# GpSimd's element work moved to ScalarE and VectorE in a hybrid attention layer

## The chip, the cores and the metric

The kernel runs on one core of a Trainium2 chip. The metric is the device time of one execution in microseconds, as the median of several executions. The engines that matter are TensorE (PE in the rows, PEld for its weight loads), VectorE (DVE), ScalarE (ACT), GpSimd (POOL) and SyncE (SP), whose queue issues most DMAs. Every engine runs its own instructions in the order in which they stand in its queue, and waits for others by semaphores.

## The reference

One layer on 1024 tokens of width 2048, in float32. Its parts, cut to what is computed:

```python
xn = rms_norm(h, norm_w)
qkv, z_a, b_raw, a_raw, u_b, v_b, z_b = split(xn @ w_in)
# group A: 8 heads of 128, gated DeltaNet in chunks of 64
q, k, v = split(silu(causal_depthwise_conv(qkv, conv_w)))       # q, k L2-normalised
beta, g = sigmoid(b_raw), -exp(a_log) * softplus(a_raw + dt_bias)
o_a = rms_norm(chunk_gated_delta_rule(q, k, v, g, beta), head_norm_w) * silu(z_a)
# group B: 8 groups of 128, gMLP in chunks of 128
v_n = layer_norm(v_b, sgu_ln_w, sgu_ln_b)
o_b = u_b * chunked_causal_sgu(v_n, w_spatial, b_spatial) * silu(z_b)
return rms_norm(h + concat(o_a, o_b) @ w_out, final_norm_w)
```

Inside a chunk the DeltaNet needs the decay mask exp(gc_i − gc_j), where gc is the running sum of g, and k, v scaled per token.

## The kernel before

**Halves and stages.** The tokens are done in two halves of 512. Each half runs `group_a` (four pairs of heads, with the recurrence of the state) and then `group_b` (eight channel groups); after both, `out_phase` does the output projection in seven products of half-size blocks, which need four sums and differences of the quarters of w_out. These are made ahead, once for each half's share, by `w_sums`, eight rounds in each `group_b`: four loads (`ws`), four VectorE operations (L833, L834, L836, L837) and four stores to the DRAM tile `wc_d`.

**Projection.** TensorE gets float32 accuracy from three products of high and low parts (L238, L239, L241). Weights come in chunks of 128 x 512: a DMA on SP's queue into `wr` (3 buffers), a cast on ScalarE into `wh` (L136, 4 buffers), a subtraction on VectorE into `wl` (L137, 4 buffers), then 12 matmuls of 512 columns. A tile is four chunks; `acc` is its sum. In the names the numbers tell tile and chunk (`wl_17_3` is chunk 3 of tile 17).

**Tasks.** What follows a tile is written as a generator that `tick()` moves on by a step. `task_gates` makes the decay masks `em` of a half: the running sums go through DRAM (`gcd`) and come back replicated (L389), GpSimd subtracts (L395), VectorE clamps (L397), ScalarE takes the exponential (L398), in four parts. `task_k`, `task_q` and `task_v` convolve (`conv`, L410 and L413), normalise (`rsqrt_`, L127 to L132) and scale per token (`kc` L486, `kd` L488, `bv` L537, em times beta L503). `task_pair` runs the recurrence of a pair, adds the part inside the chunk (`at`, L649 and L650), scales `o` by its norm (L661) and swaps it (`swap`: a 32 x 32 transpose on VectorE L425, four stores L430 and one load L433 through DRAM; for `o` on GpSimd's queue); L672 then multiplies by the gate and the result goes to `mix_d` (L673). `spatial` writes `s` (L746, L749) for group B, `task_u` multiplies it in (L755). `x_load` and its squares (L158, L159) prepare the next half's x. `finish` squares and scales the rows of the output (L950, L952) before the last factor.

**Order and buffers.** A list scheduler puts the instructions of all engines in order, with a model of the times, and takes an instruction as soon as its operands and its buffers are free. The pool `wk` gives buffers by tag, with a number of them (`cv` 3, `bv` 2, `o` 2, `gae` 3): a tile waits until the one that had its buffer before has been read for the last time. So which tag a tile has decides where its load may stand. `sp` and `at` share the two PSUM banks of `gen_bank`; therefore the matmuls at L649 of the second head of a pair wait for L746, which reads `sp`.

## Time and profile before

| | |
|---|---|
| runs | 1775.11, 1778.87, 1783.17 us; median 1778.87 |
| profiled execution | 1779.21 us, of it 1777.5 us span |
| mean granted clock of TensorE | 0.992 |
| TensorE, VectorE, ScalarE, GpSimd busy | 1728.8, 1251.7, 738.5, 263.6 us |
| DMA | 277.99 MB, mean 156 GB/s |

The span is what the profile covers of one execution; 1.7 us lie outside. Shares are averages over the whole span. Engine names in the rows are PE, PEld, DVE, ACT, POOL and SP; an SPq is SP's queue of DMA issues. An idle time is put down to what ended it, in brackets behind `<-`.

### The profile page before, as it was taken

Reading aid. Unit: us, or ns where it says so; the run is one execution under the profiler, and the core shown is the slowest. Engines: PE = TensorE matmul, PEld = TensorE weight load, DVE = VectorE, ACT = ScalarE, POOL = GpSimd, SP = SyncE. Lnnn points to the kernel's source line nnn. Section 1 sums busy time; section 2 is a strip of 40 time slices with the busy share of each in tenths; the row PEclk is TensorE's granted clock in tenths of the full one; section 3 lists DMA queues with packets and bytes.
Section 4 is the critical chain, followed back from the end, with each engine's and each line's share of the span. In section 5 each row is a group of like instructions: output and inputs, shape, how many; then the busy total and the mean of one; then the engine's idle time right before and its main releaser. Section 6 shows DMA issues by size and latency. Waiting matters only on the chain.

```text
span 1777.5 us, 27441 instructions
## 1 busy us (share of the span) xinstructions
PE 1728.8 (97%) x9334; PEld 1456.6 (82%) x9334; DVE 1251.7 (70%) x2945; ACT 738.5 (42%) x1678; POOL 263.6 (15%) x314
## 2 busy tenths in 40 slices
PE   9999999999999999998999999999989999999997
PEld 8778788888997788886878878889878888888885
DVE  7798797987747633757979789793863344767765
ACT  7543544445333222646344444532422234433454
POOL 4110131211201200203012112120020000200211
PEclk9999999999999999999999999999999999999998
DMA  7455445364458734426453645444884466766455
GB/s 239 128 134 145 108 124 144 91 169 133 132 172 260 258 108 126 130 69 153 126 134 92 164 106 149 134 116 117 248 277 133 118 188 199 223 191 193 144 190 190
DMA packets 190046, 277.99 MB, mean 156 GB/s; under 512 B 38064, under 2 KB 70864, under 8 KB 189648
## 3 DMA queue, kind: packets, MB, share of 16 engines
q1 hardware_dynamic: 185216, 263.60, 50.9%
q0 software_dynamic: 4544, 12.62, 3.0%
q8 instruction: 73, 1.20, 0.3%
q14 instruction: 69, 0.57, 0.1%
q10 hardware_dynamic: 144, 0.01, 0.0%
HBM read 220.54 MB, written 55.61 MB: 155 GB/s over the span
## 4 chain that ended last, share of the span: by engine, by line
PE 54%; DVE 9%; DMA 7%; ACT 2%; issue 2%; SPq 0%; POOL 0%; DVEq 0%; ACTq 0%; POOLq 0%
PE oa L1002 12%; PE acc L238 10%; PE acc L241 10%; PE acc L239 10%; PE vb L788 7%; DMA ws<-w_out 1%; DVE wl L137 1%; DVE cv L413 1%; DMA xres<-x_tok 1%; DMA wc_d<-ws 1%; DVE c L914 1%; PE p L621 1%; PE sp L744 1%; DMA wr<-w_in 1%; PE at L649 1%
## 5 line engine op out<-in xcount | busy, mean ns | idle before, releaser
L238 PE MATMUL acc<-xh,wh 128*128 128x512 f32 x1472 | 591.8, 402 | 1.0 <-ACT wh L136 1.0
L241 PE MATMUL acc<-xh,wl 128*128 128x512 f32 x1472 | 576.9, 392 | 7.5 <-DVE wl L137 7.5
L239 PE MATMUL acc<-xl,wh 128*128 128x512 f32 x1472 | 575.8, 391 | 0.0
L136 ACT CAST wh<-wr 128x512 fp32r<-128x512 f32 x368 | 225.7, 618 | 427.7 <-PE acc L239 270.6
L137 DVE TENSOR_TENSOR wl<-wr,wh 128x512 fp32r<-128x512 f32 x368 | 258.2, 704 | 154.2 <-ACT wh L136 151.2
L241 PEld LDWEIGHTS acc<-xh,wl 128*128 128x128 f32 x1472 | 277.1, 188 | 67.0 <-DVE wl L137 9.0
L238 PEld LDWEIGHTS acc<-xh,wh 128*128 128x128 f32 x1472 | 278.0, 189 | 57.7 <-issue 3.0
L239 PEld LDWEIGHTS acc<-xl,wh 128*128 128x128 f32 x1472 | 278.0, 189 | 51.5 <-issue 0.2
L1002 PE MATMUL oa<-who,a 128*128 128x512 f32 x864 | 267.9, 390 | 0.2 <-ACT who L136 0.2
L1002 PEld LDWEIGHTS oa<-who,a 128*128 128x128 f32 x864 | 162.6, 188 | 34.7 <-ACT who L136 0.6
L1002 PE MATMUL oa<-wlo,a 128*128 128x512 f32 x432 | 168.7, 390 | 0.6 <-DVE wlo L137 0.5
L137 DVE TENSOR_TENSOR wlo<-wro,who 128x512 fp32r<-128x512 f32 x108 | 79.4, 738 | 52.7 <-ACT who L136 52.2
L413 DVE SCALAR_TENSOR_TENSOR cv<-pc,cw,cv 128x511 f32<-128x511 f32 (+1 forms) x144 | 109.1, 758 | 9.6 <-ACT cv L410 8.2
L788 PE MATMUL vb<-whvb,xh 128*128 128x256 f32 x384 | 110.5, 288 | 0.0
L788 PE MATMUL vb<-wlvb,xh 128*128 128x256 f32 x384 | 108.6, 283 | 0.0
L788 PE MATMUL vb<-whvb,xl 128*128 128x256 f32 x384 | 108.6, 283 | 0.0
L136 ACT CAST who<-wro 128x512 fp32r<-128x512 f32 x108 | 66.6, 618 | 96.6 <-PE oa L1002 63.7
L1002 PEld LDWEIGHTS oa<-wlo,a 128*128 128x128 f32 x432 | 81.3, 188 | 18.5 <-DVE wlo L137 1.7
L566 DVE TENSOR_TENSOR fst<-fs 32x31 f32<-32x31 f32 (+15 forms) x248 | 89.3, 360 | 4.3
L568 DVE TENSOR_TENSOR fs<-fs,fst 32x31 f32<-32x31 f32 (+15 forms) x248 | 89.0, 359 | 4.1
L625 ACT ACTIVATE o<-p,g_egs 64x128 f32<-64x128 f32 x128 | 46.5, 363 | 84.3 <-DVE vz L624 81.6
L952 POOL TENSOR_TENSOR c<-c,fw 128x512 f32<-128x512 f32 x24 | 37.6, 1596 | 254.6 <-ACT sqh L950 254.6
(245 smaller groups left out, 2379.2 us busy)
## 6 DMA issues: line engine op xcount, KB each, us to landing
wr<-w_in SPq DMA_DIRECT2D x368, 256.0 KB, 3.3
ws<-w_out SPq DMA_DIRECT2D x64, 256.0 KB, 4.0
wc_d<-ws SPq DMA_DIRECT2D x64, 256.0 KB, 3.6
wro<-wc_d SPq DMA_DIRECT2D x64, 256.0 KB, 2.8
ar<-mix_d SPq DMA_DIRECT2D x56, 256.0 KB, 3.5
wrvb<-w_vb SPq DMA_DIRECT2D x48, 256.0 KB, 2.7
wro<-w_out SPq DMA_DIRECT2D x48, 256.0 KB, 2.8
xr<-x_t SPq DMA_DIRECT2D x32, 256.0 KB, 4.2
```

The source lines that it names most:

```text
L136: nc.scalar.copy(hi, src)
L137: nc.vector.tensor_tensor(lo, src, hi.bitcast(F32), op=ALU.subtract)
L238: nc.tensor.matmul(acc, hi[:, kk, :], xh, start=(k == 0), stop=False)
L239: nc.tensor.matmul(acc, hi[:, kk, :], xl, start=False, stop=(last and lo is None))
L241: nc.tensor.matmul(acc, lo[:, kk, :], xh, start=False, stop=last)
L413: nc.vector.scalar_tensor_tensor(cv[:, s:], acc[:, :T - s], w, cv[:, s:], op0=ALU.mult, op1=ALU.add)
L566: nc.vector.tensor_tensor(tv, bc(lu[:, k, k + 1:].unsqueeze(2), [32, n, m]), bc(xu[:, k:k + 1, 0:m], [32, n, m]), op=ALU.mult)
L568: nc.vector.tensor_tensor(xu[:, k + 1:, 0:m], xu[:, k + 1:, 0:m], tv, op=ALU.subtract)
L625: nc.scalar.activation(hd["o"][ra, t, :], pp[rq, :], AF.Copy, scale=gt["egs"][rq, h, t:t + 1])
L788: nc.tensor.matmul(a, l[:, tsl], r[:, k % 2, :], start=fl, stop=sp_, skip_group_check=True)
L952: nc.gpsimd.tensor_tensor(c, c, env["fw"][q], op=ALU.mult)
L1002: nc.tensor.matmul(acc[t], l[:, tsl], r[:, 0, :], start=fl, stop=sp_, skip_group_check=True)
```

## The change

Every operation of GpSimd on whole tiles goes to another engine. A product with one factor per partition and sub-block becomes four ScalarE activations with a scale per partition (`kc`, `bv`, the scaling of `o`). The subtraction ahead of the exponential becomes the bias of the exponential, with a negated copy `ngs` of the sums; the clamp on VectorE comes first, and the exponentials are then 64 of 128 x 64 in place of 8 of 128 x 512. The copy of `kq` into `wq` goes to ScalarE. Products and sums of two operands go to VectorE: half of the squares of x, em times beta, the product of `s` with `rb`, the product of `c` with `fw`. The tiles of `w_sums` change their tags from `cv` and `bv` to `o` and `gae`. GpSimd keeps memsets and DMA issues.

```diff
--- before.py
+++ after.py
@@ -156,7 +156,7 @@
                 nc.scalar.activation(xsq[hf, i], xr, AF.Square)
             else:
                 nc.scalar.activation(xr, xr, AF.Square)
-                (nc.vector, nc.gpsimd)[i].tensor_tensor(xsq[hf, i], xsq[hf, i], xr, op=ALU.add)
+                nc.vector.tensor_tensor(xsq[hf, i], xsq[hf, i], xr, op=ALU.add)
         return (xh, xl), squares
 
     def x_rstd(hf):
@@ -365,6 +365,8 @@
         nc.tensor.matmul(gp[:, 64:128], ones, gh.rearrange("p c k -> p (c k)"), start=True, stop=True)
         gc = sm.tile([P, 32], F32, tag="gs", bufs=1, name=f"gs{hf}")
         nc.scalar.copy(gc, gp[:, 0:32])
+        ngc = sm.tile([P, 32], F32, tag="ngs", bufs=1, name=f"ngs{hf}")
+        nc.scalar.activation(ngc, gp[:, 0:32], AF.Copy, scale=-1.0)
         eg, egs, ekd = g8("eg"), g8("egs"), g8("ekd")
         gam = sm.tile([P, 2, H, NT], F32, tag="gam", bufs=1, name=f"gam{hf}")
         nc.scalar.activation(fl(eg), gc, AF.Exp)
@@ -391,11 +393,12 @@
 
         gt["em"] = []
         for q in range(4):
+
             e4 = em[:, q * 8:(q + 1) * 8, :]
-            nc.gpsimd.tensor_tensor(e4, e4, bc(gc[:, q * 8:(q + 1) * 8].unsqueeze(2), [P, 8, 64]), op=ALU.subtract)
+            nc.vector.tensor_tensor(e4, e4, bc(cap.unsqueeze(1), [P, 8, 64]), op=ALU.min)
+            for a in range(8):
+                nc.scalar.activation(e4[:, a, :], e4[:, a, :], AF.Exp, bias=ngc[:, q * 8 + a:q * 8 + a + 1])
             yield 2 if q == 0 else 16
-            nc.vector.tensor_tensor(e4, e4, bc(cap.unsqueeze(1), [P, 8, 64]), op=ALU.min)
-            nc.scalar.activation(e4, e4, AF.Exp)
             gt["em"].append(e4)
 
 
@@ -483,8 +486,9 @@
         kc = wk.tile([P, NT, P], F32, tag="kc", name=f"kc{hf}_{h}")
         kd = wk.tile([P, NT, P], F32, tag="kd", bufs=3, name=f"kd{hf}_{h}")
         S4 = [P, NT, 4, 32]
-        nc.gpsimd.tensor_tensor(kc.rearrange("p t (b c) -> p t b c", c=32), z,
-                                bc(gt["eg"][:, h, :].unsqueeze(2).unsqueeze(3), S4), op=ALU.mult)
+        for t in range(NT):
+            nc.scalar.activation(kc[:, t, :].rearrange("p (b c) -> p b c", c=32), z[:, t], AF.Copy,
+                                 scale=gt["eg"][:, h, t:t + 1])
         nc.vector.tensor_tensor(kd.rearrange("p t (b c) -> p t b c", c=32), z, bc(ce.unsqueeze(2).unsqueeze(3), S4), op=ALU.mult)
         hd.update(nk=nk, c=cb, kc=kc, kd=kd)
 
@@ -500,10 +504,10 @@
         while len(gt.get("em", ())) <= h // 2 or "kd" not in hd:
             yield 1
         em = gt["em"][h // 2][:, hh * NT:(hh + 1) * NT, :]
-        nc.gpsimd.tensor_tensor(em, em, bc(hd["c"].unsqueeze(2), [P, NT, 64]), op=ALU.mult)
+        nc.vector.tensor_tensor(em, em, bc(hd["c"].unsqueeze(2), [P, NT, 64]), op=ALU.mult)
 
         wq = wk.tile([P, NT, 4, 64], F32, tag="wq", bufs=2, name=f"wq{hf}_{h}")
-        nc.gpsimd.tensor_copy(wq[:, :, 1:3, :], kq[:, 1, :].rearrange("p (t c i) -> p t c i", c=2, i=64))
+        nc.scalar.copy(wq[:, :, 1:3, :], kq[:, 1, :].rearrange("p (t c i) -> p t c i", c=2, i=64))
         yield 1
         ga = gen_bank(f"ga{hf}_{h}").rearrange("p (t i) -> p t i", i=P)
         for t in range(NT):
@@ -534,8 +538,9 @@
         while "nk" not in hd:
             yield 1
         bv = wk.tile([P, NT, P], F32, tag="bv", name=f"bv{hf}_{h}")
-        nc.gpsimd.tensor_tensor(bv.rearrange("p t (b c) -> p t b c", c=32), z, bc(hd["nk"].unsqueeze(2).unsqueeze(3), [P, NT, 4, 32]),
-                                op=ALU.mult)
+        for t in range(NT):
+            nc.scalar.activation(bv[:, t, :].rearrange("p (b c) -> p b c", c=32), z[:, t], AF.Copy,
+                                 scale=hd["nk"][:, t:t + 1])
         hd["bv"] = bv
 
     def task_z(hf, h, st, pr, acc):
@@ -658,7 +663,8 @@
             nc.vector.tensor_scalar(hd["ssq"], hd["ssq"], EPS, EPS * P, op0=ALU.add, op1=ALU.mult)
             nc.vector.tensor_tensor(so, so, hd["ssq"], op=ALU.add)
             rsqrt_(ro, so, [P, NT], f"o{nm}")
-            nc.gpsimd.tensor_tensor(o, o, bc(ro.unsqueeze(2), [P, NT, P]), op=ALU.mult)
+            for t in range(NT):
+                nc.scalar.activation(o[:, t, :], o[:, t, :], AF.Copy, scale=ro[:, t:t + 1])
             yield W_SO0
             y = hd["ut"].rearrange("p t d -> p (t d)")
             hd["ot"] = swap(y, o.rearrange("p t d -> p (t d)"), y, f"o{nm}", nc.gpsimd, True)
@@ -746,7 +752,7 @@
         nc.vector.scalar_tensor_tensor(s1, sp, lnw[:, g:g + 1], bc(brow[:, g, :].unsqueeze(1), [P, NT, P]),
                                        op0=ALU.mult, op1=ALU.add)
         s1f = s1.rearrange("p t i -> p (t i)")
-        nc.gpsimd.tensor_tensor(s1f, s1f, sb["rb"], op=ALU.mult)
+        nc.vector.tensor_tensor(s1f, s1f, sb["rb"], op=ALU.mult)
         sb[g] = s1f
 
     def task_u(hf, g, sb, acc):
@@ -827,7 +833,7 @@
         for cb, k in ck:
             q = {}
             for i, b in enumerate(((1, 1), (0, 1), (0, 0), (1, 0))):
-                q[b] = wk.tile([P, 1, T], F32, tag=("cv", "bv")[i // 2], bufs=(3, 2)[i // 2], name=f"ws{cb}_{k}_{i}")
+                q[b] = wk.tile([P, 1, T], F32, tag=("o", "gae")[i // 2], bufs=(2, 3)[i // 2], name=f"ws{cb}_{k}_{i}")
                 nc.sync.dma_start(q[b], w_quarter(b, cb, k))
             yield 5
             nc.vector.tensor_tensor(q[1, 1], q[1, 1], q[0, 1], op=ALU.subtract)
@@ -949,7 +955,7 @@
             sq = wk.tile([P, T], F32, tag="rb", bufs=1, name=f"sqh{n}_{cb}_{t}")
             nc.scalar.activation(sq, c, AF.Square, accum_out=ss[:, q:q + 1])
             if not last:
-                nc.gpsimd.tensor_tensor(c, c, env["fw"][q], op=ALU.mult)
+                nc.vector.tensor_tensor(c, c, env["fw"][q], op=ALU.mult)
                 return
             others = [i for i in range(4) if i != q]
             yield 1
```

In the rows of the changed kernel line numbers are 3 to 6 higher than in the kernel before from the gates on. The numbers at the end of names are the scheduler's and differ between the two.

**SP, during the swap of the last pair of the first half.** `wr` are weights of the projection, `ws` and `wc_d` loads and stores of the sums, `mix_d<-o_3_0` and `mix_d<-o_3_1` what the two heads of the pair store after their swap. Before:

```order
L831 DMA ws_5_2_7000<-w_out 128x512
L831 DMA ws_5_3_7002<-w_out 128x512
L831 DMA ws_6_0_7113<-w_out 128x512
L187 DMA wr_34_0_6365<-w_in 128x512
L840 DMA wc_d<-ws_5_0_6996 128x512
L840 DMA wc_d<-ws_5_1_6998 128x512
L187 DMA wr_34_1_6383<-w_in 128x512
L673 DMA mix_d_132<-o_3_0_5711 128x512
L840 DMA wc_d<-ws_5_2_7000 128x512
```

Changed, around the store of the second head:

```order
L187 DMA wr_42_3_6630<-w_in 128x512
L187 DMA wr_35_0_6649<-w_in 128x512
L679 DMA mix_d_132<-o_3_1_5835 128x512
L187 DMA wr_35_1_6667<-w_in 128x512
L837 DMA ws_0_1_6501<-w_out 128x512
L187 DMA wr_35_2_6689<-w_in 128x512
L846 DMA wc_d<-ws_0_0_6499 128x512
L846 DMA wc_d<-ws_0_1_6501 128x512
L187 DMA wr_35_3_6730<-w_in 128x512
L846 DMA wc_d<-ws_0_2_6503 128x512
L846 DMA wc_d<-ws_0_3_6505 128x512
```

Before, the first head's store stands in the midst of the sixth round of sums; in the changed kernel the first round is stored behind the second head's store, and only four loads of sums stand ahead of that.

**VectorE, around L672 of the first head** (L678 in the changed kernel), whose operand `ut` is the load of the swap. Before:

```order
L137 TENSOR_TENSOR wl_41_0_6287<-wr_41_0_6284,wh_41_0_6286 128x512
L137 TENSOR_TENSOR wl_41_1_6312<-wr_41_1_6309,wh_41_1_6311 128x512
L833 TENSOR_TENSOR ws_5_0_6996<-ws_5_0_6996,ws_5_1_6998 128x512
L834 TENSOR_TENSOR ws_5_1_6998<-ws_5_1_6998,ws_5_2_7000 128x512
L836 TENSOR_TENSOR ws_5_2_7000<-ws_5_2_7000,ws_5_0_6996 128x512
L137 TENSOR_TENSOR wl_41_2_6330<-wr_41_2_6327,wh_41_2_6329 128x512
L672 SCALAR_TENSOR_TENSOR o_3_0_5711<-ut_3_0_5703,hnw,z_6_4785 128x512
L837 TENSOR_TENSOR ws_5_3_7002<-ws_5_3_7002,ws_5_2_7000 128x512
L746 SCALAR_TENSOR_TENSOR s_0_6156<-sp_0_6151,lnw,brow 128x512
L137 TENSOR_TENSOR wl_41_3_6349<-wr_41_3_6346,wh_41_3_6348 128x512
```

Changed:

```order
L137 TENSOR_TENSOR wl_41_1_6410<-wr_41_1_6407,wh_41_1_6409 128x512
L137 TENSOR_TENSOR wl_41_2_6428<-wr_41_2_6425,wh_41_2_6427 128x512
L678 SCALAR_TENSOR_TENSOR o_3_0_5803<-ut_3_0_5795,hnw,z_6_4868 128x512
L752 SCALAR_TENSOR_TENSOR s_0_6251<-sp_0_6246,lnw,brow 128x512
L755 TENSOR_TENSOR s_0_6251<-s_0_6251,rb_715 128x512
L137 TENSOR_TENSOR wl_41_3_6447<-wr_41_3_6444,wh_41_3_6446 128x512
L761 TENSOR_TENSOR s_0_6251<-s_0_6251,acc_32_6037 128x512
L655 TENSOR_TENSOR o_3_1_5835<-o_3_1_5835,at_3_1_6319 128x512
```

The sums `ws_5` are gone from ahead of L672 and from between it and L746 (L752); the product with `rb` stands behind it.

**VectorE, around `wl_17_3` of the second half,** with the masks `em`, the convolved tile `cv_16` and the products `gl`, `gae` of the first pair. Before:

```order
L413 SCALAR_TENSOR_TENSOR cv_16_8533<-pc_16_8531,cw,cv_16_8533 128x509
L514 TENSOR_TENSOR gl_0_8493<-ga_0_8484,em_8327 128x256
L521 TENSOR_TENSOR gae_0_8496<-ga_0_8484,em_8327 64x4x64 x2
L415 SCALAR_TENSOR_TENSOR cv_16_8533<-tails,cw,cv_16_8533 128x3
L137 TENSOR_TENSOR wl_17_3_8545<-wr_17_3_8542,wh_17_3_8544 128x512
L137 TENSOR_TENSOR wl_24_0_8567<-wr_24_0_8564,wh_24_0_8566 128x512
```

Changed, first ahead of `wl_17_3`, then ahead of `wl_24_0`:

```order
L137 TENSOR_TENSOR wl_17_2_8636<-wr_17_2_8633,wh_17_2_8635 128x512
L398 TENSOR_TENSOR em_8427<-em_8427,cap 128x512
L132 SCALAR_TENSOR_TENSOR ce_1_8529<-rst_k_1_8531,ce_1_8529 128x4
L398 TENSOR_TENSOR em_8427<-em_8427,cap 128x512
L130 TENSOR_TENSOR rst_k_1_8531<-ce_1_8529 128x4
L407 TENSOR_TENSOR pc_16_8651<-acc_16_8499,rb_8174 128x512
L131 TENSOR_TENSOR rst_k_1_8531<-rst_k_1_8531,rsm_k_1_8532 128x4
L137 TENSOR_TENSOR wl_17_3_8665<-wr_17_3_8662,wh_17_3_8664 128x512
```

And further on, up to `wl_24_0`:

```order
L525 TENSOR_TENSOR gae_0_8616<-ga_0_8604,em_8427 64x4x64 x2
L507 TENSOR_TENSOR em_8427<-em_8427,cc_1_8528 128x256
L663 TENSOR_SCALAR ssq_0_8621<-ssq_0_8621 128x4
L518 TENSOR_TENSOR gl_1_8705<-ga_1_8696,em_8427 128x256
L525 TENSOR_TENSOR gae_1_8708<-ga_1_8696,em_8427 64x4x64
L416 SCALAR_TENSOR_TENSOR cv_16_8653<-pc_16_8651,cw,cv_16_8653 128x511
L418 SCALAR_TENSOR_TENSOR cv_16_8653<-tails,cw,cv_16_8653 128x1
L416 SCALAR_TENSOR_TENSOR cv_16_8653<-pc_16_8651,cw,cv_16_8653 128x510
L418 SCALAR_TENSOR_TENSOR cv_16_8653<-tails,cw,cv_16_8653 128x2
L416 SCALAR_TENSOR_TENSOR cv_16_8653<-pc_16_8651,cw,cv_16_8653 128x509
L418 SCALAR_TENSOR_TENSOR cv_16_8653<-tails,cw,cv_16_8653 128x3
L137 TENSOR_TENSOR wl_24_0_8687<-wr_24_0_8684,wh_24_0_8686 128x512
```

`wl_17_3` has moved ahead of the convolution and the masks' products; those now stand between it and `wl_24_0`, and two clamps stand ahead of it.

## Rows read from the trace of the kernel before

**Rows 1.** Page part 1: busy us, share of the span, instructions, by engine

```profile
PE 1728.8 (97%) x9334; PEld 1456.6 (82%) x9334; DVE 1251.7 (70%) x2945; ACT 738.5 (42%) x1678; POOL 263.6 (15%) x314
```

**Rows 2.** Timeline of PE around 823 us: start us, length us, instruction [idle before]

```profile
823.09 0.39 PE L238 MATMUL acc<-xh,wh 128*128 128x512 f32 x1
823.32 0.39 PE L239 MATMUL acc<-xl,wh 128*128 128x512 f32 x1
829.28 0.80 PE L241 MATMUL acc<-xh,wl 128*128 128x512 f32 x1 [5.58 <-DVE wl L137]
```

**Rows 3.** Waits of PE: us in total, times, longest us

```profile
PE at L649 <- DVE s L746: 10.7, 2, 5.6
PE acc L241 <- DVE wl L137: 7.5, 3, 5.6
```

**Rows 4.** Windows: busy us of PE, PEld, DVE, ACT, POOL; PEclk, DMA share, GB/s

```profile
575.00:585.00 10.00, 4.93 (x22) 4.53 (x23) 6.81 (x11) 2.75 (x10) 2.20 (x2) 0.66 0.84 280
514.00:604.00 90.00, 83.20 (x468) 71.59 (x467) 66.24 (x160) 31.83 (x81) 13.38 (x15) 0.96 0.80 258
```

**Rows 5.** Timeline around the stop at 574 us: POOL, VectorE and PE

```profile
560.18 1.04 POOL L661 TENSOR_TENSOR o<-o,ro 128x512 f32<-128x512 f32 x1 [83.58 <-DVE ro L132]
572.30 0.57 POOL L433 DMA_DIRECT2D ut<-swapo  x1 [6.64 <-DMA swapo<-ut]
...
560.22 1.54 DVE L833 TENSOR_TENSOR ws<-ws,ws 128x512 f32<-128x512 f32 x1 [0.57 <-DMA ws<-w_out]
577.91 0.75 DVE L672 SCALAR_TENSOR_TENSOR o<-ut,hnw,z 128x512 f32<-128x512 f32 x1 [1.59 <-DMA ut<-swapo]
579.18 0.74 DVE L746 SCALAR_TENSOR_TENSOR s<-sp,lnw,brow 128x512 f32<-128x512 f32 x1
...
580.07 2.05 PE L649 MATMUL at<-ut,gae 128*128 128x128 f32 x8 [5.63 <-DVE s L746]
```

**Rows 6.** The swap's load, L433: timeline row of a quiet pair; landing

```profile
256.62 0.56 POOL L433 DMA_DIRECT2D ut<-swapo  x1 [3.09 <-DMA swapo<-ut]
...
DMA to landing us min/median/max: 2.6/3.4/6.5
```

**Rows 7.** Page part 6, DMA issues: count, KB each, median us to landing

```profile
wr<-w_in SPq DMA_DIRECT2D x368, 256.0 KB, 3.3
ws<-w_out SPq DMA_DIRECT2D x64, 256.0 KB, 4.0
wc_d<-ws SPq DMA_DIRECT2D x64, 256.0 KB, 3.6
```

**Rows 8.** Groups of ACT by line: busy us, mean ns, idle before

```profile
L136 ACT CAST wh<-wr 128x512 fp32r<-128x512 f32 x368 | 225.7, 618 | 427.7 <-PE acc L239 270.6 <-DMA wr<-w_in 82.7 <-issue 31.1
L655 ACT ACTIVATE so<-o 128x128 f32<-128x128 f32 x64 | 19.8, 310 | 24.1 <-DVE rst_o L131 11.9 <-DVE o L650 10.8
L398 ACT ACT_TABLE_LOAD x3 | 3.8, 1283 | 0.1
```

**Rows 9.** Timeline of POOL, VectorE and ACT ahead of the stop at 823 us

```profile
816.93 4.50 POOL L395 TENSOR_TENSOR em<-em,gs 128x512 f32<-128x512 f32 x4 [4.77 <-DMA em<-gcd]
...
818.44 1.00 DVE L132 SCALAR_TENSOR_TENSOR ce<-rst_k,ce 128x4 f32<-128x4 f32 x1
828.54 1.28 DVE L137 TENSOR_TENSOR wl<-wr,wh 128x512 fp32r<-128x512 f32 x2
...
824.10 1.28 ACT L398 ACT_TABLE_LOAD   x1
825.40 0.63 ACT L398 ACTIVATE em<-em 128x512 f32<-128x512 f32 x1
```

**Rows 10.** Groups of VectorE by line: busy us, mean ns

```profile
L159 DVE TENSOR_TENSOR xsq<-xsq,xr 128x512 f32<-128x512 f32 x14 | 9.5, 681 | 0.0
L132 DVE SCALAR_TENSOR_TENSOR ce<-rst_k,ce 128x4 f32<-128x4 f32 x48 | 10.1, 211 | 1.2
```

**Rows 11.** Group of POOL by line: busy us, mean ns, idle before

```profile
L952 POOL TENSOR_TENSOR c<-c,fw 128x512 f32<-128x512 f32 x24 | 37.6, 1596 | 254.6 <-ACT sqh L950 254.6
```

## The prediction

> **What bounds the kernel now.** I read the shares of the engines first, then what TensorE waited for, then the timeline around its longest waits, and last the DMA table. TensorE is busy for 97% of the span, VectorE for 70%, ScalarE for 42% and GpSimd for 15% [rows 1]. In an undisturbed stretch TensorE starts a matmul of 512 columns every 0.23 us [rows 2], so a chunk of a projection tile (12 matmuls) takes 2.76 us, and TensorE sets the time wherever nothing is late. What a change on other engines can win is therefore no more than TensorE's gaps: 1777.5 − 1728.8 = 48.7 us, of which the start and the last chain behind TensorE are untouched here. The list of waits puts names to the largest gaps. Two stops of some 5 us, one in each half, wait for the VectorE step at L746, 10.7 us together, and 7.5 us go to late low parts of weights, 5.6 of them in one stop [rows 3]. A stop costs more than its length, since the granted clock sinks behind it: in the ten microseconds around the first stop TensorE was busy for 4.93 us at a mean granted clock of 0.66 [rows 4], which is 4.93 × 0.34 = 1.7 us lost on top. GpSimd's own 264 us matter only where somebody waits for them or is slowed by them.
>
> **The swap of the last head pair (−13 us).** The first stop is a chain [rows 5]. GpSimd scales o_3_0 at 560.18. VectorE's sum L833 starts beside it, takes 1.54 us where this operation takes about 0.7, and stands ahead of the transpose that starts the swap. The swap goes through DRAM: GpSimd waits 6.64 us for its four stores before it can issue the load at 572.30, and L672, which uses the load, starts 5.61 us later. L746 follows at 579.18 behind L672 and one more sum, and TensorE goes on at 580.07 after a gap of 5.63 us. In a quiet pair the same wait was 3.09 us, and such a load lands in a median 3.4 us [rows 6]. The reason is the DMA load of the sums: between 514 and 604 us the DMA engines are 80% busy at 258 GB/s [rows 4].
>
> The change takes the buffers of the sums from cv and bv, which are free early, and gives them o and gae, which the last pair still holds. In the order of the changed kernel the sums (loads and VectorE work) stand behind this swap, with only a few loads ahead of it. So the wait for stores goes down by 6.64 − 3.4 = 3.2 us (I take 3.4, a load's median, as the upper of the two quiet figures), the load by 5.61 − 3.4 − 0.3 (to start behind it) = 1.9 us, and the two sums that stood in front leave, 0.7 us for each and the 0.8 by which the first was slowed: 7.3 us in all, some 1 us of which the hoisted loads of x and w_out may keep. That exceeds the gap of 5.63. Next late are the weights, whose supply is priced below, and a rest of some 0.5 us per half. The saving: 10.7 + 2 × 1.7 − 2 × 0.5 = 13.1 us. Its bounds are 14 (nothing left) and 6 (the early loads still disturb the swap and half remains).
>
> **The sums behind the swap (+4 us).** This is what the change may cost. Per half there are 32 loads and 32 stores of 256 KB (16.8 MB), and on the same in-order queue of SP stand 25 loads of weights (6.6 MB) among them; before, loads of wrvb stood there too. TensorE eats 25 chunks in 25 × 2.76 = 69 us. For that the DMA would have to move 23.4 MB in 69 us, 339 GB/s. Before, 258 GB/s at 80% busy is 322 GB/s at full share, thus 73 us. Each round of four tiles is also a chain: load 4.0, sums about 1.5 and half a microsecond of issue, store 3.6 [rows 7], some 9.6 us, thus 77 us for eight rounds. Had it gone at 258 GB/s as before, it would be 91 us. Behind a waiting store or load of the sums stand the weights, and for those VectorE's subtraction and TensorE wait. Slack: three raw and four converted chunks, of which six are ahead, 6 × 2.76 = 16.6 us, less landing 3.3 [rows 7], cast 0.6 [rows 8], subtraction 0.7 and 1 of waits, about 11 us. So 73 or 77 us (4 to 8 us behind) cost nearly nothing, and 91 us (22 behind) cost 11 us per half. I take 2 us per half, since the chain of 77 us is the nearest to what the order shows, and single late rounds will be longer than the mean; ends 0 and 22 in all.
>
> **The decay masks of the first pair (−2 us).** The stop of 5.58 us at 829.28 [rows 2] waits for the subtraction wl_17_3, which VectorE started at 828.54. Ahead of it GpSimd's four subtractions ran from 816.93 for 4.5 us, during which VectorE's 128x4 steps took 1.00 us at 818.44 [rows 9] where the mean of that line is 0.21 [rows 10]. After, VectorE has wl_17_3 ahead of the cv steps and is not slowed, so it comes at about 821. But the next subtraction, wl_24_0, stands behind four clamps, two em products, gl, gae and three cv steps: from 817.35 some 12 to 13 us of VectorE work, ending near 830, and TensorE wants it at 823.5 + 2.76 + 0.5 = 826.8. So the stop moves by one tile and shrinks from 5.6 to about 3.5 us. Both VectorE and ScalarE now stand in order behind the landing of em, for which only GpSimd waited. Bounds −6 (no stop) and +3 (em lands later). Switching between tables took 1.28 us here, and the next activation started 1.30 us after the start of the load [rows 9]; eight more switches, mean 1.283 [rows 8], are 10 us of ScalarE, nearly all beside TensorE. The Trainium skill, "ScalarE: Activation LUTs", section "What ACT_TABLE_LOAD costs", adds a drain of 1.38 us to each, 2.66 us in all; the trace does not agree, since no such pause stands between load and activation. By the page this term would be about 0 instead of −2.
>
> **Moved element work, elsewhere (−1 us).** VectorE takes L159 (14 × 0.68 = 9.5 us), the spatial product (16 × 0.68 = 10.9), em times beta (16 at most 0.68, 10.9) and L952 (24 × 0.68 = 16.3, 24 times 1.6 on GpSimd before [rows 11]), 48 us at most, with 0.681 as the mean of the same operation at L159 [rows 10]. Even with nothing given back that is 1300 us, 73%. It gets back what GpSimd's work beside it costs today (the 1.54 at L833, the 1.00 at L132), a like amount by my estimate. ScalarE gets 3 × 16 × 4 = 192 activations of 128x128 (59 us at the 0.310 of L655), 16 copies (10 us), 64 exponentials for 8 (at most 20 us) and 10 us of tables [rows 8]: about 838 us, 47%. The cover is the conversion buffers, some 8 us ahead of TensorE. If ScalarE waits longer than that in order for a swap, the casts behind it are late. For the small gaps in group A I take −1, with bounds −5 and +5.
>
> **The end (+1 us).** In the output phase four of the 24 products stand on VectorE ahead of the last chains, up to 3 × 0.68 = 2 us, of which I take half; the last chain behind TensorE has none. Memsets and the DMA issues of the swap stay on GpSimd, which then is nearly free for them: no cost.
>
> **The sum.** −13 + 4 − 2 − 1 + 1 = −11 us. The profiled run took 1779.2 us (span 1777.5 and 1.7 around it), within 0.3 of the median of 1778.9, so no correction: 1768 us.
>
> **Rivals.**
> *The weights starve behind the sums* (slower). If the eight rounds don't overlap with the weights but follow one another at 12.5 us (the 9.6 us chain and one chunk's load behind it), the stage is 100 us, 31 behind, less 11 of slack, 20 us per half and 1.7 of clock: 43 in place of 4, so 1807 us. From 258 GB/s (91 us) it is 25 in place of 4, 1789. It decides from 10.9 us a round (18 behind, 7 us and 1.7 per half), where the gain is gone. For it speaks that the queue is in order and that 339 GB/s has no row; against it the small number of weights per round (three) and the slack. Chance 0.15.
> *The stop stays in part.* The early loads of x and w_out fill the DMA queues while the swap is under way and half of the saving is lost: −11 + 7 = −4, 1775 us. Chance 0.17.
> *ScalarE becomes the late one.* The bv scaling waits in its queue for the swap of v, and exponentials with tables stand ahead of casts; at half a microsecond for each of 16 heads 8 us are lost, 1776 us. Against it: ScalarE waits for swaps of q and k in the same way today, and its casts spend 270.6 us waiting for TensorE to free their buffers [rows 8], so they have room. Chance 0.13.
> *Everything goes.* No lag, no stop at the first pair and smaller gaps: −13 − 6 − 3 + 1 = −21, 1758 us. Here a page bears: the Trainium skill, "SBUF — State Buffer", section "A bandwidth-pool intuition that's wrong (but worth ruling out)", gives about 358 GB/s between HBM and a core. By that the stage would be 65 us and cost nothing, 1764 us by my sum; the trace shows no stretch at that rate. Chance 0.13.
> *The forecast*, 1762 to 1774 us: chance 0.42.
>
> **How the numbers follow.** Half a per cent, 8.9 us, is about what a measurement of this kernel can tell from no change: faster is below 1770, slower above 1788. Faster: 0.13 and most of the forecast's 0.42 (0.35), with 0.02 from the rest: 0.50. Slower: the first rival beyond 1788, 0.14. Same: 0.36. The range from 1756 to 1788 leaves out the worse part of the first rival and the tail of the best case.
>
> **What would show it.** Right: no stop over 2 us near 574 and 1300 us, the GpSimd wait ahead of the swap's load at 3 to 4 us, sums running from about 575 to 655 us, a stop of 3 to 4 us one tile later at 826 us, VectorE's L132 at 0.16 us there. Wrong: stops of TensorE on wl or wh between 600 and 660 us, with SP waiting for wc_d or ws; new waits on wh in group A behind scaled copies.

## The result, and the profile after

The changed kernel takes 1751.8 us (1750.7 to 1754.2) against 1777.0 us before, a ratio of 0.985 with a 95% interval of 0.983 to 0.987. That is 25 us, where 11 were forecast, and 4 us below the end of the range. The profiled execution took 1754.2 us, its span 1752.5.

Page part 1 of the changed kernel answers to [rows 1]:

```profile
PE 1724.6 (98%) x9334; PEld 1457.0 (83%) x9334; DVE 1222.7 (70%) x3015; ACT 823.5 (47%) x1952; POOL 95.3 (5%) x172
```

GpSimd lost 168 us and ScalarE gained 85. VectorE took over 54 instructions of 128x512 and 16 of 128x256 (some 44 us) and is nonetheless 29 us shorter. Most of what it got back is seen by comparing each of its instructions with the median of its line and shape in the same trace. What instructions take beyond that median, counted where it is over 0.1 us, is called VectorE's excess from here on: before, it adds up to 66.7 us, of which 66.3 fall on instructions that run beside a memset or element instruction of GpSimd; after, it is 0.0.

The waits of TensorE (us in total, times, longest), first two of before that [rows 3] did not show, then the same and two more of the changed kernel:

```profile
PE ds L632 <- DVE vz L624: 4.0, 10, 0.9
PE wp L611 <- DVE wq L612: 2.8, 3, 1.1
```

```profile
PE acc L241 <- DVE wl L137: 11.5, 8, 2.8
PE oa L1008 <- ACT wk L136: 1.1, 1, 1.1
PE ds L637 <- DVE vz L629: 0.6, 3, 0.2
PE wp L616 <- DVE wq L617: 0.6, 1, 0.6
```

The stops for L746 are gone from the list. The many short waits of the recurrence (`ds` for `vz`, `wp` for `wq`) are nearly gone too. The waits for low parts of weights have grown from 7.5 to 11.5 us.

Where the 25 us lie is read by aligning the two traces at the same matmul. The table gives, for the profiled executions, how much longer (+) or shorter (−) a stage is than before; times are those of before, both halves together. The first 55 us and what follows the last matmul are left out (0.7 us at most). Each column is one execution; single executions of the changed kernel lie within 4 us, those of e1 within 15. The row below `rest` is VectorE's excess in group A, in us. The columns to the right are the experiments below.

| stage (us of before) | forecast | after | e1 | e2 | e3 | e9 | e5 | e10 | e6 | e4 | e7 | e8 | e11 | e12 |
|---|---|---|---|---|---|---|---|---|---|---|---|---|---|---|
| masks (85–111, 811–847) | −2 | +1.0 | −1.3 | −1.8 | +1.8 | +0.3 | −6.4 | −1.2 | −1.8 | −0.8 | −0.3 | +5.6 | +4.8 | −2.3 |
| group A (111–532, 847–1259) | −1 | −13.1 | +5.7 | −12.7 | −6.7 | −7.4 | −2.0 | −6.4 | −11.9 | −13.1 | −12.8 | −12.2 | −11.7 | −13.3 |
| swap (532–634, 1259–1350) | −13 | −16.7 | −14.3 | −2.0 | −16.7 | −15.2 | −15.9 | −1.3 | −16.7 | −15.5 | −15.0 | −15.2 | −15.3 | −8.4 |
| sums (634–705, 1350–1434) | +4 | +12.2 | +14.8 | 0.0 | +12.6 | +0.6 | +6.7 | 0.0 | +11.0 | 0.0 | +1.3 | +2.0 | +1.0 | +22.8 |
| output phase (1434 to the last matmul) | +1 | −5.7 | −0.5 | −5.5 | −3.0 | −5.0 | −4.5 | −1.7 | −0.6 | −3.1 | −4.3 | −3.3 | −4.9 | −4.8 |
| rest (55–85, 705–811) | | −3.4 | −0.6 | −3.4 | −3.5 | −3.3 | −2.2 | −1.8 | −3.3 | −3.2 | −3.2 | −3.3 | −2.3 | −3.2 |
| VectorE's excess in A (24.1 before) | | 0.0 | 23.2 | 1.0 | 12.5 | 11.2 | 19.7 | 3.8 | 0.0 | 0.4 | 0.5 | 0.5 | 0.5 | 0.7 |
| **span, profiled** | | 1752.5 | 1781.7 | 1752.7 | 1762.3 | 1748.0 | 1752.9 | 1765.7 | 1754.3 | 1742.3 | 1743.8 | 1751.4 | 1749.0 | 1769.2 |
| **median time** | 1768 | 1751.8 | 1774.8 | 1756.2 | 1758.4 | 1751.0 | 1755.5 | 1766.7 | 1755.8 | 1743.7 | 1746.1 | 1753.1 | 1750.3 | 1770.9 |

**The swap**, timeline of the changed kernel, against [rows 5] (GpSimd, VectorE, TensorE):

```profile
566.27 0.56 POOL L436 DMA_DIRECT2D ut<-swapo  x1 [3.90 <-PE acc L241]
```

```profile
569.60 0.74 DVE L678 SCALAR_TENSOR_TENSOR o<-ut,hnw,z 128x512 f32<-128x512 f32 x1
570.38 0.75 DVE L752 SCALAR_TENSOR_TENSOR s<-sp,lnw,brow 128x512 f32<-128x512 f32 x1
```

```profile
571.28 1.13 PE L654 MATMUL at<-ut,gae 128*128 128x128 f32 x8
```

The wait ahead of the load is 3.90 us instead of 6.64 (it now ends with TensorE's L241, the four stores having landed at 565.61), the multiplication starts 3.3 us behind the load instead of 5.6, nothing stands between it and L752, and TensorE goes through without a stop. The windows of the changed kernel (columns as in [rows 4]) show the clock at 1.00 behind it, and the sums running later at up to 0.87 of DMA share:

```profile
575.00:585.00 10.00, 10.00 (x51) 8.43 (x50) 6.60 (x22) 4.08 (x11) 2.93 (x4) 1.00 0.59 157
600.00:660.00 60.00, 60.00 (x279) 50.14 (x277) 35.47 (x56) 13.60 (x22) 0.00 (x0) 1.00 0.87 284
660.00:680.00 20.00, 16.66 (x65) 13.02 (x64) 9.68 (x16) 3.72 (x6) 0.00 (x0) 0.91 0.79 252
```

**The sums**, VectorE and TensorE around the stop at 664 us:

```profile
664.10 0.69 DVE L839 TENSOR_TENSOR ws<-ws,ws 128x512 f32<-128x512 f32 x1 [4.72 <-DMA ws<-w_out]
666.56 0.69 DVE L137 TENSOR_TENSOR wl<-wr,wh 128x512 fp32r<-128x512 f32 x1
```

```profile
667.30 0.50 PE L241 MATMUL acc<-xh,wl 128*128 128x512 f32 x1 [2.84 <-DVE wl L137]
```

VectorE waits 4.72 us for a load of a sum, in the seventh of the eight rounds, and the subtraction of weights behind it comes at 666.56. The cast of these weights had ended at 661.35. In the second half a stop of 2.76 us stands at the same round.

**The masks in the first half**, VectorE and TensorE:

```profile
90.60 0.69 DVE L398 TENSOR_TENSOR em<-em,cap 128x512 f32<-128x512 f32 x1 [4.08 <-DMA em<-gcd]
```

```profile
92.76 0.50 PE L241 MATMUL acc<-xh,wl 128*128 128x512 f32 x1 [1.80 <-DVE wl L137]
98.33 0.80 PE L241 MATMUL acc<-xh,wl 128*128 128x512 f32 x1 [1.21 <-DVE wl L137]
```

The clamp waits 4.08 us in order for the landing of `em`, and the subtraction behind it is late. The load was issued at 81.4 us, 2.2 later than before, and took up to 8.6 us to land instead of 6.5.

### The profile page after: what moved, and what is told of

It is laid out like the page before. It is cut to its first block, busy times and chain, and to the rows that moved or that the text cites. A ratio compares the mean times of both kernels' runs of the same rounds, so it can differ in the third digit from the quotient of the medians.

```text
span 1752.5 us, 27530 instructions
## 1 busy us (share of the span) xinstructions
PE 1724.6 (98%) x9334; PEld 1457.0 (83%) x9334; DVE 1222.7 (70%) x3015; ACT 823.5 (47%) x1952; POOL 95.3 (5%) x172
## 4 chain that ended last, share of the span: by engine, by line
PE 78%; DMA 9%; DVE 8%; issue 2%; ACT 2%; SPq 1%; POOL 0%; DVEq 0%; ACTq 0%; POOLq 0%
PE oa L1008 15%; PE acc L238 14%; PE acc L241 14%; PE acc L239 14%; PE vb L794 8%; DMA wr<-w_in 2%; DMA ws<-w_out 2%; DMA wc_d<-ws 2%; PE ds L637 1%; DVE wl L137 1%; PE p L626 1%; DVE cv L416 1%; PE first L307 1%; PE first L306 1%; PE first L308 1%
## 5 line engine op out<-in xcount | busy, mean ns | idle before, releaser
L241 PE MATMUL acc<-xh,wl 128*128 128x512 f32 x1472 | 579.5, 394 | 11.5 <-DVE wl L137 11.5
L241 PEld LDWEIGHTS acc<-xh,wl 128*128 128x128 f32 x1472 | 278.2, 189 | 73.4 <-DVE wl L137 15.2
L137 DVE TENSOR_TENSOR wl<-wr,wh 128x512 fp32r<-128x512 f32 x368 | 250.3, 684 | 96.3 <-ACT wh L136 93.4
L136 ACT CAST who<-wro 128x512 fp32r<-128x512 f32 x108 | 66.7, 618 | 92.7 <-PE oa L1008 71.6
L137 DVE TENSOR_TENSOR wlo<-wro,who 128x512 fp32r<-128x512 f32 x108 | 73.9, 687 | 50.0 <-ACT who L136 49.4
L1008 PEld LDWEIGHTS oa<-wlo,a 128*128 128x128 f32 x432 | 81.1, 188 | 16.8
L571 DVE TENSOR_TENSOR fst<-fs 32x31 f32<-32x31 f32 (+15 forms) x248 | 81.0, 327 | 4.4
L573 DVE TENSOR_TENSOR fs<-fs,fst 32x31 f32<-32x31 f32 (+15 forms) x248 | 81.0, 327 | 4.2
L794 PEld LDWEIGHTS vb<-whvb,xh 128*128 128x128 f32 x384 | 73.7, 192 | 0.2
L794 PEld LDWEIGHTS vb<-wlvb,xh 128*128 128x128 f32 x384 | 73.7, 192 | 0.0
```

Of the source, the lines that this page charges most:

```text
L136: nc.scalar.copy(hi, src)
L137: nc.vector.tensor_tensor(lo, src, hi.bitcast(F32), op=ALU.subtract)
L241: nc.tensor.matmul(acc, lo[:, kk, :], xh, start=False, stop=last)
L571: nc.vector.tensor_tensor(tv, bc(lu[:, k, k + 1:].unsqueeze(2), [32, n, m]), bc(xu[:, k:k + 1, 0:m], [32, n, m]), op=ALU.mult)
L573: nc.vector.tensor_tensor(xu[:, k + 1:, 0:m], xu[:, k + 1:, 0:m], tv, op=ALU.subtract)
L794: nc.tensor.matmul(a, l[:, tsl], r[:, k % 2, :], start=fl, stop=sp_, skip_group_check=True)
```

## Experiments

In front of each: the kernel that it changes. Medians and spans stand in the table.

**e1: the buffers alone** (on the kernel before).

```diff
-tag=("cv", "bv")[i // 2], bufs=(3, 2)[i // 2]
+tag=("o", "gae")[i // 2], bufs=(2, 3)[i // 2]
```

> The kernel before with one edit: the tiles of w_sums in the buffers of o and gae; all element work stays on GpSimd. Theory A (the two stops at L649 come from the sums' DMA load beside the swap, the late subtractions at the end of the sums from their squeezed rounds, and both hang on the buffers alone): the stops of 5.6 and 5.0 us go (with the clock 8.5 us per half), stops of about 3 us appear in the eighth round of sums in each half (6 us per half with the clock), net -5 us: 1772 us. Rival B (the stops come from GpSimd's scaling of o and from VectorE being slowed by it): the stops stay, and the late rounds come on top: 1789 us.

1774.8 us, ratio 0.998 (0.996 to 1.000), single runs from 1768 to 1783. Theory A holds for both stages: swap −14.3, sums +14.8. What it does not explain are +5.7 us in group A of the profiled execution, which was 9 us above the median; longer waits at L593 for ScalarE stand there, and why is left open.

**e2: everything but the buffers** (on the changed kernel; e1's edit undone).

```diff
-tag=("o", "gae")[i // 2], bufs=(2, 3)[i // 2]
+tag=("cv", "bv")[i // 2], bufs=(3, 2)[i // 2]
```

> The changed kernel with one edit undone: the tiles of w_sums again in the buffers of cv and bv; GpSimd has no element work. Theory A (what the gain in group A, at the masks and at the end is worth comes from the moved element work alone, some 20 us, and the swap's stops from the buffers): the stops at L649 come back (17 us for both halves), the late rounds of sums go (12 us): 1752 + 5 = 1757 us. Rival B (the stops were GpSimd's): they stay away, 1740 us.

1756.2 us. The stops are back and the late sums are gone:

```profile
PE at L654 <- DVE s L752: 9.5, 2, 4.9
PE acc L241 <- DVE wl L137: 5.2, 4, 1.9
```

So the stops belong to the buffers; without GpSimd's work the stage is only 2.0 us shorter in all. Where the stop of the first half comes from is seen on GpSimd and VectorE:

```profile
565.13 0.56 POOL L436 DMA_DIRECT2D ut<-swapo  x1 [3.68 <-PE acc L241]
```

```profile
569.50 0.69 DVE L839 TENSOR_TENSOR ws<-ws,ws 128x512 f32<-128x512 f32 x1 [3.66 <-DMA ws<-w_out]
571.58 0.69 DVE L840 TENSOR_TENSOR ws<-ws,ws 128x512 f32<-128x512 f32 x1 [1.39 <-DMA ws<-w_out]
573.51 0.74 DVE L678 SCALAR_TENSOR_TENSOR o<-ut,hnw,z 128x512 f32<-128x512 f32 x1
```

The wait ahead of the load is as short as in the changed kernel. But the load lands 5.9 us after its issue (2.9 in the changed kernel), and L678 comes another 2.5 us later, behind sums that waited for their own loads. Group A, the output phase and the rest stay within 0.4 us of the changed kernel; the masks are 2.8 us shorter. By the medians the moved element work is worth 22 us, and the buffers add 4: 14.7 won at the swap and 12.2 lost at the sums in the profiled executions (whose spans differ by 0.2 us only, since the masks of e2 are the shorter ones).

**e3 and e9: GpSimd works, nobody waits** (on the changed kernel, and on e4). Four lines of this kind, for `kc`, `bv`, `o` and the copy of `wq`:

```diff
+jk = wk.tile([P, NT, P], F32, tag="jk", bufs=1, name=f"jk{hf}_{h}")
+nc.gpsimd.tensor_tensor(jk.rearrange("p t (b c) -> p t b c", c=32), z,
+                        bc(gt["eg"][:, h, :].unsqueeze(2).unsqueeze(3), S4), op=ALU.mult)
```

> The changed kernel, and in addition GpSimd does four of its former operations per head (the products of kc, bv and o, the copy of wq) on the same operands into a scratch tile that nobody reads. Theory C (the gain in group A is VectorE no longer slowed while GpSimd works): VectorE's instructions beside GpSimd become long again and most of the 13 us of group A go back: 1762 us. Rival D (the gain is that the chain no longer waits for GpSimd's slower instruction): nobody waits for the scratch, 1752 us.

> The kernel with the sums split three and five (1743.7 us), and GpSimd's four former operations per head on a scratch tile that nobody reads, as in the earlier run on the changed kernel. It repeats that run where no late sums lie beside it. Theory C (VectorE slowed by GpSimd's work costs some 6 us of TensorE's time, nearly all in group A): 1750 us, with +3 us in group A of each half. If the earlier difference belonged to its profile alone: 1744 us.

1758.4 us, 6.6 more than the changed kernel; 1751.0 us, 7.3 more than e4 (5.7 by the two ratios to the kernel before, 0.984 and 0.980, which was run beside each). Group A takes 6.4 and 5.7 us more, with no reader of the scratch tile; of the waits listed for e9 only those for `ones` at the start end with a GpSimd instruction. VectorE's excess is back at 16.8 and 15.0 us, all of it beside GpSimd. e3's profiled execution was 5.6 us above its median, e9's 1.2 below. A step of VectorE in e9 with the one ahead of it, and the GpSimd instruction beside it:

```profile
1039.22 0.34 DVE L579 TENSOR_TENSOR fst<-fs 32x192 f32<-32x192 f32 x1
1039.60 1.12 DVE L581 TENSOR_TENSOR fs<-fs,fst 32x192 f32<-32x192 f32 x1
```

```profile
1039.47 1.04 POOL L550 TENSOR_TENSOR jv<-pc,nk 128x512 f32<-128x512 f32 x1 [17.92 <-DMA pc<-swapv]
```

The second VectorE step has the first one's shape and takes 1.12 us in place of 0.34; it ends 0.21 us behind the end of GpSimd's (1040.72 and 1040.51). The Trainium skill, "SBUF — State Buffer", section "SBUF: two separate sides", says that the two engines share a pair of ports that is locked for a whole instruction when both need it, the other standing still; these rows agree with it. TensorE pays where VectorE stands in its chain:

```profile
PE ds L645 <- DVE vz L637: 3.0, 9, 0.7
```

So theory C is shown, for the 12.5 and 11.2 us of excess that these runs bring back to group A: half of it, 0.51 and 0.53 us for each, became TensorE's time (for e9 over e4's excess of 0.4).

**e5: the four operations back on GpSimd, in use** (on the changed kernel). For `kc`, and likewise for `bv`, `o` and the copy of `wq`:

```diff
-for t in range(NT):
-    nc.scalar.activation(kc[:, t, :].rearrange("p (b c) -> p b c", c=32), z[:, t], AF.Copy,
-                         scale=gt["eg"][:, h, t:t + 1])
+nc.gpsimd.tensor_tensor(kc.rearrange("p t (b c) -> p t b c", c=32), z,
+                        bc(gt["eg"][:, h, :].unsqueeze(2).unsqueeze(3), S4), op=ALU.mult)
```

> The changed kernel with four operations per head given back to GpSimd (the products of kc and bv, the scaling of o, the copy of wq), this time with their results in use. The run with the same operations on a scratch tile was 6.6 us slower than the changed kernel, 6.4 us of it in group A. Theory C+D (the other half of group A's 13 us is the chain waiting for GpSimd's slower instructions): another 6 us go, 1765 us, with TensorE's waits for wq and vz back. Theory C alone (slowing of VectorE by any GpSimd work is all): as with the scratch tile, 1758 us.

1755.5 us (single executions 1754.6 to 1766.1), less than either theory gave, but not for their reason: group A lost 11.1 of its 13.1 us, where e3 had lost 6.4. This doesn't show that waiting for GpSimd's results costs the other 4.7, since VectorE's excess in group A is 19.7 us here and 12.5 in e3: for each microsecond of it 0.56 us were lost, nearly as in e3. What waiting alone costs no run separates. The short waits are back as before:

```profile
PE ds L635 <- DVE vz L627: 4.4, 10, 0.9
PE wp L614 <- DVE wq L615: 2.8, 3, 1.1
```

What made it cheap are the masks (−6.4 instead of +1.0) and shorter stops at the sums (+6.7). `em` had landed by 87.5 us instead of 90.6 in the first half, and nobody waited for it; which of the four brought that is open.

**e10: the four operations alone** (on the kernel before: e5's diff the other way round, for the same four).

> The kernel before with one part of the change: the products of kc and bv, the scaling of o and the copy of wq on ScalarE; masks, squares, em times beta, the spatial product, the product with fw and the buffers of the sums as before. Theory C+D (these four hold most of group A's 13 us, by the slowing and by the waits): group A 9 to 11 us shorter, stops of the swap as before or 1 us shorter, 1767 us. If each of the other GpSimd operations slows VectorE as much: group A 4 to 6 us shorter, 1773 us.

1766.7 us, ratio 0.992 (0.990 to 0.995), as theory C+D gave it in sum, but not by stages: group A is 6.4 us shorter, where C+D had 9 to 11 and the other theory 4 to 6; the rest comes from the end, the masks, the swap and the stretch from 55 to 85 us, 1 to 2 us each. VectorE's excess in group A is down to 3.8 us; at 0.5 us for each microsecond of the 20.3 that went, group A would be some 10 us shorter. Of the 6.4 us 5.6 lie in the second half and 0.8 in the first, where one new stop of 2.0 us (and its clock) waits for ScalarE at 185 us. The swap's stops stand.

**e6: masks and the product with `fw` back on GpSimd** (on the changed kernel).

```diff
+nc.gpsimd.tensor_tensor(e4, e4, bc(gc[:, q * 8:(q + 1) * 8].unsqueeze(2), [P, 8, 64]), op=ALU.subtract)
+yield 2 if q == 0 else 16
 nc.vector.tensor_tensor(e4, e4, bc(cap.unsqueeze(1), [P, 8, 64]), op=ALU.min)
-for a in range(8):
-    nc.scalar.activation(e4[:, a, :], e4[:, a, :], AF.Exp, bias=ngc[:, q * 8 + a:q * 8 + a + 1])
-yield 2 if q == 0 else 16
+nc.scalar.activation(e4, e4, AF.Exp)
...
-    nc.vector.tensor_tensor(c, c, env["fw"][q], op=ALU.mult)
+    nc.gpsimd.tensor_tensor(c, c, env["fw"][q], op=ALU.mult)
```

> The changed kernel with two edits undone that lie in stages of their own: the subtraction of the masks on GpSimd with the exponential in 8 instructions, and the product of c with fw on GpSimd. Theory (masks: VectorE is slowed in the second half, VectorE and ScalarE wait in order for the landing of em in the first): the stage from 85 to 111 us wins 4 to 6 us, the one from 811 to 847 us loses 5 us. End: if the 4 us at the end come from the product of c with fw, they go; if they come from what stands ahead of it, they stay. 1752 to 1756 us.

1755.8 us. The output phase gives back 5.1 of its 5.7 us, and VectorE's excess in it is back at 15.8 us (16.1 before, 0.0 in the changed kernel). TensorE's longest stop there, for `wk`, takes 2.8 us (3.4 before, 1.1 in the changed kernel). Over all runs this stage stands at −0.5 to −1.7 where the product with `fw` is on GpSimd (e1, e6, e10) and at −3.0 to −5.7 where it is on VectorE, so the product has a part in it, of 1 to 5 us. At the masks the expectation fell: the second half kept its −5.8 us, and the first still has a stop, of 3.3 us; GpSimd waits until 89.4 us for `em` there. The second half's stop of 5.6 us is shorter in e1 (3.2) and in e2 (1.7) too, which share no edit; several delays added up in it, and which of them decided is open.

**e4: the sums split** (on the changed kernel).

```diff
-tag=("o", "gae")[i // 2], bufs=(2, 3)[i // 2]
+tag=(("cv", "bv") if k < 3 else ("o", "gae"))[i // 2], bufs=((3, 2) if k < 3 else (2, 3))[i // 2]
```

> The changed kernel with the first three of eight rounds of sums in the buffers of cv and bv, the other five in those of o and gae. If the stops of 2.8 us come only because the delay of the rounds adds up over eight of them, five rounds behind the swap end before the slack is used up, and three ahead of it are over before the swap starts: 12 us less, 1740 us. If the early rounds fall into the swap, the stops at L649 come back in part: 1748 to 1757 us.

1743.7 us, ratio 0.980 (0.979 to 0.982): faster than both kernels. The swap keeps its gain and the late sums are gone (0.0). The waits of TensorE for low parts are the masks' alone now:

```profile
PE acc L241 <- DVE wl L137: 4.1, 3, 1.8
```

This is what the delay of the rounds adding up to the slack would give: five rounds end before it is used.

**e12: the additions of the sums on GpSimd** (on the changed kernel; all four alike).

```diff
-nc.vector.tensor_tensor(q[1, 1], q[1, 1], q[0, 1], op=ALU.subtract)
+nc.gpsimd.tensor_tensor(q[1, 1], q[1, 1], q[0, 1], op=ALU.subtract)
```

> The changed kernel (1752 us) with the four additions of each round of sums on GpSimd instead of VectorE; loads, stores and buffers as they are. The late low parts in the eighth round cost 12 us in both halves together. Theory E (the subtractions stand in VectorE's queue behind an addition that waits for the load of a sum; the converted weights lie ready beside it): without it VectorE goes on, the stops at 667 and 1379 us go, 12 us less: 1740 us, or 1743 with VectorE slowed a little. Theory F (the weights themselves are late, since SP's queue holds them behind the stores of the sums): GpSimd's additions take longer, the stores wait longer, the stops grow: 1758 us or more.

1770.9 us. The gain forecast by theory E did not come, and the stops of theory F did: VectorE no longer stands behind a load, and TensorE now waits for the weights themselves.

```profile
PE acc L238 <- ACT wh L136: 18.4, 9, 5.9
PE acc L241 <- DVE wl L137: 5.0, 5, 1.6
```

SP's queue waits for the slower additions (L839 takes 1.35 us on GpSimd, 0.69 on VectorE) ahead of its stores, and the weights stand behind these. The longest of these stops, at 622 us, falls into the stage of the swap, whose first half therefore shows 0.0; the sums cost some 31 us in all. In the changed kernel VectorE's wait came last at the stop; the next two casts ended at 664.06 and 666.70, each as its load landed. So the run does not refute E for the stop of the changed kernel, since it made the additions twice as long as well; it shows that the queue was not far behind.

**e7 and e8: two tries on e4.** e7 has the first edit, e8 both.

```diff
-nc.sync.dma_start(out[r0:r0 + P, o_ * T:(o_ + 1) * T], h)
+(nc.sync if n == LAST else nc.gpsimd).dma_start(out[r0:r0 + P, o_ * T:(o_ + 1) * T], h)
...
-for c in range(2):
-    nc.gpsimd.dma_start(em[c * 64:(c + 1) * 64], gcd[c].partition_broadcast(64))
+for q in range(4):
+    for c in range(2):
+        nc.gpsimd.dma_start(em[c * 64:(c + 1) * 64, q * 8:(q + 1) * 8, :],
+                            gcd[c, q * 8:(q + 1) * 8, :].partition_broadcast(64))
```

> The kernel with the sums split three and five, and in addition the output stores of all but the last product on GpSimd's queue. If the stop of 2 us ahead of the last product comes from 16 stores that keep SP's queue for 10 us ahead of the weights, it goes: 3 us less, 1740 us. If the weights are late for another reason, 1744 us.

> As the one before, and the masks' loads em in quarters (8 DMAs for 2), so that the first clamp and exponentials wait for a quarter's landing only. If the stops at the masks (3.3 us in the first half, 1.8 in the second) come from VectorE and ScalarE standing in order behind that landing, most go: 5 us less with the clock, 1736 us. If DMAs on GpSimd's queue cost more than the quarters win: 1741 us or more.

1746.1 and 1753.1 us: neither gained. e7 missed both of its branches, e8 fell on its second. In e7 the stop for `wk` went, and one of 1.7 us for the weights behind it came. In e8 eight issues take GpSimd 4.1 us where two took 1.0, and the stop of the first half grew to 5.2 us.

**e11: the loads of `em` on SP's queue** (on e4).

```diff
-nc.gpsimd.dma_start(em[c * 64:(c + 1) * 64], gcd[c].partition_broadcast(64))
+nc.sync.dma_start(em[c * 64:(c + 1) * 64], gcd[c].partition_broadcast(64))
```

> The kernel with the sums split three and five (1743.7 us), and the two loads of the masks em issued on SP's queue in place of GpSimd's. If the stops at the masks come from the landing of em (90.6 us in the changed kernel, after an issue at 81.4 on GpSimd's queue), and SP's queue lands it 3 us earlier, the stage from 85 to 111 us wins 3 us and the one of the second half 1 to 2: 1739 us. If the wait for gcd on SP's queue holds back weights: 1746 us or more.

1750.3 us, the second branch. In the first half the clamps start at 86.8 us, 2.9 earlier than in e4, and nothing is won: stops of 1.3, 0.7 and 2.0 us stand between 81 and 90 us. In the second half TensorE stops for 5.3 us at 813 us, for a cast. SP's queue waits 3.3 us for `gcd` ahead of these weights, and on ScalarE the cast stands behind sixteen exponentials (808.24 to 812.17 us); which of the two decided is open.

## Why the prediction was wrong

**The term that failed: "moved element work, elsewhere (−1 us)".** It measured −13.1 us in group A and −3.4 in the rest, outside its bounds of −5 and +5. The step weighed VectorE by its share (73% after) and looked for stops among the two largest waits, [rows 3]. In group A TensorE stood idle for 11.4 us before and for 2.0 after: eleven waits of 0.36 to 1.06 us, 8.3 us together, and shorter ones, none of which I counted as something to win. (The other 4 us of the gain do not show as idle time.) The recurrence is a chain through TensorE, VectorE and, once a head, GpSimd; there a VectorE step that lasts 1.1 instead of 0.34 us can hold up TensorE. The prediction had the mechanism in hand, in L833's 1.54 us and L132's 1.00, and used it only to show that VectorE's load stays level. e3 and e9, where nobody waits for GpSimd's results, show the mechanism alone: 0.51 and 0.53 us of TensorE's time for each microsecond of VectorE's excess. At that rate the 24.1 us of before come to 12 or 13 us, nearly all of the 13.1; this is an estimate from those two runs. The 3.4 us of the rest are not taken apart: 1.8 of them came with the four operations of e10, ahead of 85 us.

**The end (+1 us)** had the wrong sign, −5.7. The products of `fw` were priced on VectorE's queue; that they slow VectorE while on GpSimd (by 16 us in this stage) was left out. Put back (e6), the stage loses 5.1 us. The stage differs by up to 2.7 us between kernels with the same code in it (e3, e4 and the changed kernel), so not all of it is the product's.

**The swap (−13 us)** was right in place and cause, and measured −16.7; the waits shrank as worked out (6.64 to 3.90, 5.61 to 3.33). e1 and e2 show from both sides that the buffers do it. But the largest part of the sum, 3.2 us for the stores, is not what the stop hangs on: in e2 that wait is 3.68 us and the stop is there, by the slower load and the sums ahead of L678.

**The sums (+4 us)** were right in mechanism and mis-sized: +12.2. A round was forecast at 9.6 us and took 10.9 on the mean (the first stores of the first and the eighth round were issued at 600.1 and 676.7), so eight rounds take some 87 us, not 77. Against 69 us of weights that is 18 behind, beyond the slack of 11; so the seventh round meets TensorE in both halves, and in the first half stops of 2.8 and 0.5 us with the fall of the clock (0.91 between 660 and 680 us) cost 5.6. The loads of `ws` landed in 4.8 us instead of 4.0. The prediction's own rule (nothing up to the slack, all beyond it) gives 17 us in both halves for 10.9 us a round; 2 us per half rested on the chain of 77 us alone.

**The masks (−2 us)** measured +1.0 from −5.6 and +6.6. In the second half the stop came at the tile that was forecast and was 1.65 us instead of 3.5. Why is open: e6 gives the subtractions back to GpSimd, and the stop does not return. In the first half, for which the sum has no term, the bound "em lands later" came true: 90.6 us against 86.3, and VectorE and ScalarE stood in order behind it.

**The rivals.** "Everything goes" (1758 us, 0.13) came nearest, though its sums were to cost nothing: they cost 12 us, and small waits gave back more than it had. "The weights starve" came true in its mechanism, at the 10.9 us a round from which it decides, though it cost 12 us and not 17. The stop did not stay in part, and ScalarE was not late (1.1 us of waits for `wh`, 1.0 before). What "Everything goes" says last, that the trace shows no stretch at the rate it takes, holds for the 44 us slices of the page (277 GB/s at most), but not for shorter ones: before, 369 GB/s were moved from 10 to 20 us, and 350 from 1730 to 1740.

That the total missed by only 14 us is partly luck: the sums and the masks cost 11 us more than forecast, and group A with the rest, the end and the swap won 26 more.

## What to carry to other kernels

Where TensorE is bound and a recurrence runs through VectorE, add up the short waits of TensorE by what ended them before pricing an edit, and count an engine that slows VectorE by the instructions of the chain that it overlaps, not by shares. A buffer tag is a schedule: moving loads behind a swap frees the swap and squeezes the loads, and a split between early and late rounds took both gains (e4). Slack is a threshold, so compare the backlog with it round by round.

## What the runs showed of the hardware

GpSimd's work on scratch of 61 us (95 to 156 us busy) lengthened VectorE by 14 to 16 us and the kernel by 6 to 7 us, with no data between them (e3, e9). In group A each microsecond that VectorE lost beside GpSimd cost the kernel 0.51 to 0.56 us (e3, e9, e5, and the kernel before against the changed one); in the output phase, with 16 us lost in e6, it was about 0.3. ScalarE's activations with a scale per partition and table loads in the changed kernel, groups by line (busy us, mean ns, idle before):

```profile
L490 ACT ACTIVATE kc<-pc,g_eg 128x128 f32<-128x128 f32 x64 | 21.1, 390 | 0.1
L667 ACT ACTIVATE o<-o,ro 128x128 f32<-128x128 f32 x64 | 20.4, 389 | 14.4 <-DVE ro L132 14.4
L400 ACT ACT_TABLE_LOAD x7 | 9.0, 1283 | 3.7 <-DMA em<-gcd 3.6
```

An activation of 128x128 took 390 ns here, not the 310 of [rows 8], a line without a scale by partition, so the 59 us of the prediction become 75; all in all ScalarE rose by 85 us, where 100 had been forecast. DMA moved 284 GB/s for 60 us at 0.87 of its share, short of the 339 that weights and sums together would have needed.
